# Second output projection of six channel groups as seven block products, with weight differences formed by GpSimd in layer 0

## The chip, the cores and the metric

The kernel runs on one core of one Trainium2 chip. The core has a matrix engine (TensorE, PE in the profile), a vector engine (VectorE, DVE), an engine for activation functions (ScalarE, ACT), a general engine (GpSimd, POOL) and a queue engine that issues DMA transfers (SyncE, SP). Each engine executes its own list of instructions in order, and they wait for each other by semaphores. Working memory is SBUF; matmuls write to PSUM, which has eight banks here, each 128 partitions of 512 float32. The metric is the device time of one execution in microseconds.

## The reference: what is computed

A two-layer encoder over 16 meta tokens and 256 input tokens of width 2048, all in float32, one sequence. Layer 0 mixes with gated linear attention and stick-breaking attention. Layer 1, the layer of this change, is a Mamba-2 mixer:

```python
proj = jnp.einsum('btd,de->bte', h, w_in)                 # 2048 -> 10304
z, xbc, dt_raw = _split(proj, ODD_SPLITS)
xbc = jax.nn.silu(_causal_depthwise_conv(xbc, conv_w, conv_b))
...
y = _ssd(xs, bs, cs, dt, a_log, d_skip)                   # 4096 channels in 8 groups of 512
y = _rms_norm_groups(y * jax.nn.silu(z), norm_w, SSM_GROUPS)
return jnp.einsum('bte,ed->btd', y, w_out)                # 4096 -> 2048
```

After it come the residual and a layer norm. The change concerns the last einsum, the output projection: for each of the eight groups the 256 kept tokens times 512 channels are multiplied with a block of 512 x 2048 of `w_out`, and the eight results are added.

## The kernel before

**Number format.** Matmuls run on `float32r` operands. To keep float32 accuracy each operand is split in a high part (an ACT copy to `float32r`, L159) and a residue (a subtraction, L160, on DVE or on POOL), and each product is three matmuls: high x high, high x low, low x high (`three`, L176 to 180). Weights arrive as `raw` tiles of 128 x 2048 (1 MB), three buffers; each half of 1024 columns is split into a pair of tiles `whi` and `wlo`, five buffers each. `split_half` (L162) gives the second half of every third unit of layer 1, from unit 24 on, to POOL.

**Units.** The work is a list of weight units, `L0` with 104 and `L1` with 112. An input unit of layer 1 (`in_unit`, L182) computes 128 output channels for all tokens: 16 k-tiles times three matmuls of up to 272 columns, in four quarters of 12. For each SSM group g there are ten: B, C, four of x, four of z. An output unit (`out1_unit`, L505) multiplies group g's 512 channels with 512 columns of `w_out`: two token halves times four k-tiles times three matmuls of 128 x 512, so 24, into two PSUM banks, and then two DVE instructions (L503) scale each bank by the RMS factor `rr` of its tokens (tokens lie on partitions there) and add it to `acc`. `L1` is ssd(0), ssd(1), and then for g = 2 to 7 ssd(g) followed by out1(g - 2), and at the end out1(6) and out1(7).

**Side work.** After each quarter of an input unit, and at four places of an output unit, `tick` (L109) lets every pending generator emit its next step. `post_*` reads a finished unit from PSUM; for B, C and x it is the convolution (`conv`, L1062: one ACT instruction and three of DVE, all reading the PSUM bank). `decay1` (L1099) prepares the decay matrix `M`, and `mix_ssd` (L1236) does the chunk matmuls, multiplies with the SiLU gate on POOL (L1266), weights and splits the result into `yh` and `yl` (L1268, L1269; two buffers each) and computes the RMS factor (L1279 to 1289). `tail` (L1292) runs the last five output units with the layer norm, all of token half 0 before half 1.

**What sets the order.** Instructions are recorded in the order of the code; a planner then orders every engine's list by that order as a priority and by a simulated readiness. `post_*` and additions to `acc` are recorded with raised priority. `pin` keeps the order among some matmuls, and `keep_order` that of DVE and ACT at the end. Weight loads, the small round trips of `to_tokens` in layer 0 (L594) and the broadcast of decays (L1089) all go through SP's queue. PSUM has four banks `pj` for unit results, two `po` and two `z` for side work.

## Time and profile before

Three runs gave 1382.5, 1382.53 and 1383.26 us, median 1382.53. The page shows one profiled execution; it gives the span from its first to its last instruction, and no time of its own for that execution.

| what | value |
|---|---|
| median of the runs | 1382.53 us |
| profiled execution, span | 1385.0 us |
| profiled execution, own time | not given on the page |
| PE busy | 1374.1 us (99%) |
| DVE busy | 1030.8 us (74%) |
| ACT busy | 768.3 us (55%) |
| POOL busy | 263.1 us (19%) |
| DMA | 256.73 MB, mean 185 GB/s |

A line of the page's instruction groups names the code line, the engine, the operation, the tiles written and read, the shape and the count, then the busy time and the mean duration of one, then the idle time of the engine just before it and what ended it. The stretch from 0 to about 679 us is layer 0, the rest layer 1; group 7's last input unit ends at about 1305 us. PE's durations are those of pipelined instructions, so that the distance between two starts, and not the length of one, is what a matmul costs.

### The profile page before, as it was taken

How to read it: one execution, taken by the hardware profiler on the slowest of the kernel's cores; microseconds unless marked ns; L12 is line 12 of the kernel's file. 1: busy time of each engine (PE TensorE's matmuls, PEld its weight loads, DVE VectorE, ACT ScalarE, POOL GpSimd, SP SyncE). 2: the span in 40 equal slices, each digit the busy share in tenths (PEclk: the TensorE clock that was granted, in tenths of full speed). 3: DMA queues.
4: the chain of work that ended last, by engine and by line, in shares of the span. 5: the costliest groups of instructions: out<-in, count | busy, mean ns of one | idle time of the engine just before them, and what ended most of it. 6: DMA issues, size and time to landing. Idle time of an engine off the chain costs nothing.

```text
span 1385.0 us, 26232 instructions
## 1 busy us (share of the span) xinstructions
PE 1374.1 (99%) x10643; PEld 1323.9 (96%) x10643; DVE 1030.8 (74%) x1762; ACT 768.3 (55%) x1141; POOL 263.1 (19%) x253
## 2 busy tenths in 40 slices
PE   9999999999999999999999999999999999999998
PEld 8999999999999999999999999899898999989986
DVE  7858576576565674568899999787877778867687
ACT  6646455355345544556587667656565655656551
POOL 0000100100101100004401143331322323133221
PEclk9999999999999999999999999999999999999999
DMA  9656446546455545554355655465555555455561
GB/s 329 209 172 201 163 163 206 169 155 227 153 173 171 169 161 191 172 165 161 123 183 197 231 181 205 169 244 182 209 177 195 190 191 222 169 198 183 181 214 61
DMA packets 61945, 256.73 MB, mean 185 GB/s; under 512 B 26176, under 2 KB 29056, under 8 KB 33408
## 3 DMA queue, kind: packets, MB, share of 16 engines
q1 hardware_dynamic: 61104, 254.27, 53.3%
q8 instruction: 83, 1.36, 0.4%
q10 hardware_dynamic: 720, 0.79, 0.2%
q14 instruction: 38, 0.31, 0.1%
HBM read 249.29 MB, written 5.74 MB: 184 GB/s over the span
## 4 chain that ended last, share of the span: by engine, by line
PE 94%; DVE 4%; DMA 1%; issue 1%; POOL 0%; ACT 0%; SPq 0%; ACTq 0%; DVEq 0%; POOLq 0%
PE pj L179 25%; PE pj L178 25%; PE pj L180 25%; PE pj L494 4%; PE pj L496 4%; PE pj L495 4%; PE po L1255 1%; PE po L631 1%; DVE wlo L160 1%; PE po L1193 0%; DMA raw<-in_wts 0%; DVE M L1125 0%; PE z L1143 0%; DVE xt L1070 0%; DVE acc L503 0%
## 5 line engine op out<-in xcount | busy, mean ns | idle before, releaser
L178 PE MATMUL pj<-xhi,whi 128*128 128x272 f32 (+4 forms) x2560 | 732.1, 286 | 1.7 <-ACT xhi L330 0.8
L179 PE MATMUL pj<-xlo,whi 128*128 128x272 f32 (+4 forms) x2560 | 730.8, 286 | 0.0
L180 PE MATMUL pj<-xhi,wlo 128*128 128x272 f32 (+4 forms) x2560 | 730.1, 286 | 0.0
L159 ACT ACTIVATE whi<-raw 128x1024 fp32r<-128x1024 f32 (+2 forms) x434 | 449.2, 1039 | 398.3 <-PE pj L179 326.3
L160 DVE TENSOR_TENSOR wlo<-raw,whi 128x1024 fp32r<-128x1024 f32 (+2 forms) x405 | 503.4, 1247 | 209.6 <-ACT whi L159 199.6
L178 PEld LDWEIGHTS pj<-xhi,whi 128*128 128x128 f32 x2560 | 482.6, 189 | 4.3 <-ACT whi L159 1.1
L179 PEld LDWEIGHTS pj<-xlo,whi 128*128 128x128 f32 x2560 | 482.6, 189 | 1.2 <-issue 0.6
L180 PEld LDWEIGHTS pj<-xhi,wlo 128*128 128x128 f32 x2560 | 482.6, 189 | 0.8 <-issue 0.8
L178 PE MATMUL pj<-mixh,whi 128*128 128x272 f32 x384 | 111.0, 290 | 0.0
L180 PE MATMUL pj<-mixh,wlo 128*128 128x272 f32 x384 | 110.7, 289 | 0.0
L179 PE MATMUL pj<-mixl,whi 128*128 128x272 f32 x384 | 110.7, 288 | 0.0
L160 POOL TENSOR_TENSOR wlo<-raw,whi 128x1024 fp32r<-128x1024 f32 x29 | 73.1, 2520 | 193.7 <-ACT whi L159 193.7
L494 PE MATMUL pj<-whi,yh 128*128 128x512 f32 (+1 forms) x240 | 93.3, 389 | 0.0
L495 PE MATMUL pj<-wlo,yh 128*128 128x512 f32 (+1 forms) x240 | 92.6, 386 | 0.0
L496 PE MATMUL pj<-whi,yl 128*128 128x512 f32 (+1 forms) x240 | 92.2, 386 | 0.0
L261 POOL TENSOR_TENSOR gr<-gr,gsc 128x1088 f32<-128x1088 f32 x6 | 15.4, 2574 | 303.6 <-ACT gsc L260 303.6
L179 PEld LDWEIGHTS pj<-mixl,whi 128*128 128x128 f32 x384 | 72.4, 188 | 0.2
L180 PEld LDWEIGHTS pj<-mixh,wlo 128*128 128x128 f32 x384 | 72.3, 188 | 0.0
L178 PEld LDWEIGHTS pj<-mixh,whi 128*128 128x128 f32 x384 | 72.2, 188 | 0.2
L503 DVE SCALAR_TENSOR_TENSOR acc<-pj,rr,acc 128x512 f32<-128x512 f32 (+1 forms) x65 | 46.5, 733 | 13.9 <-PE pj L496 13.9
L496 PEld LDWEIGHTS pj<-whi,yl 128*128 128x128 f32 x240 | 45.1, 188 | 9.2
L494 PEld LDWEIGHTS pj<-whi,yh 128*128 128x128 f32 x240 | 45.1, 188 | 8.9
(347 smaller groups left out, 1462.4 us busy)
## 6 DMA issues: line engine op xcount, KB each, us to landing
raw<-in_wts SPq DMA_DIRECT2D x212, 1024.0 KB, 4.8
ebc<-edr SPq DMA_DIRECT2D x8, 1664.0 KB, 6.4
raw<-in_wts SPq DMA_DIRECT2D x9, 256.0 KB, 6.3
vdr<-vt SPq DMA_DIRECT2D x8, 256.0 KB, 5.2
vt<-vdr SPq DMA_DIRECT2D x32, 64.0 KB, 2.4
hacc<-in_xT SPq DMA_DIRECT2D x7, 272.0 KB, 5.3
early<-in_wts SPq DMA_DIRECT2D x2, 512.0 KB, 7.7
vdr<-vt SPq DMA_DIRECT2D x8, 128.0 KB, 3.4
```

The source lines that it names most:

```text
L159: self.nc.scalar.activation(hi, src, AF.Copy)
L160: eng.tensor_tensor(lo, src, hi.bitcast(F32), op=ALU.subtract)
L178: mm(ps, whi, xhi, start=first, stop=False)
L179: mm(ps, whi, xlo, start=False, stop=False)
L180: mm(ps, wlo, xhi, start=False, stop=last)
L261: mul(c, c, e, op=ALU.mult)
L494: mm(ps, yh[:, kk, tt], hi[:, k, :], start=kk == 0, stop=False)
L495: mm(ps, yh[:, kk, tt], lo[:, k, :], start=False, stop=False)
L496: mm(ps, yl[:, kk, tt], hi[:, k, :], start=False, stop=kk == 3)
L503: self.nc.vector.scalar_tensor_tensor(a, ps, r[:, t : t + 1], a, op0=ALU.mult, op1=ALU.add)
L631: mm = lambda r, a, b, start=False, stop=False: self.nc.tensor.matmul(o[:, r], a, b, start=start, stop=stop, skip_group_check=True)
L1255: pin(mm(ov[p][i * 64 : (i + 1) * 64, jj, t0:S], xd[:, s, h * 64 : (h + 1) * 64], M[:, h, c0:c1], start=(s, jj) == (0, 0), stop=False, **gk,))
```

## The change

For groups 0 to 5 the output projection is done by Strassen's scheme in Winograd's form. For a group and a half q of the 2048 output columns, `y` (256 tokens x 512 channels) and the weights (512 x 1024) are cut into 2 x 2 blocks. With A the blocks of `y` and B those of the weights, seven products replace eight: A11 B11, A12 B21, S2 T2, S3 T3, S1 T1, (-A22) T4 and S4 B22, where S1 = A21 + A22, S2 = S1 - A11, S3 = A11 - A21, S4 = A12 - S2, and T1 = B12 - B11, T3 = B22 - B12, T2 = B22 - T1, T4 = T2 - B21. Each product is 128 x 256 times 256 x 512, six matmuls of 128 x 512. There are 6 x 2 x 7 = 84 products.

- **Order of units.** `L1` is now ssd(0) to ssd(7) without a break, then out1(6) and out1(7). The products stand between quarters of the input units: the first of group g after quarter 64 + 40 g of layer 1 (unit 16 + 10 g), the others 20/7 quarters apart. Each product is followed by one addition to `acc`.
- **Weight differences.** The blocks lie in DRAM a second time, in the order B11, B12, B22, B21 (`_pack`). In layer 0 a generator `quad_sums` loads 24 tiles of 1 MB through SP, forms T1 to T4 in place by four subtractions of 128 x 512 each on POOL, and stores the tile to DRAM through SP.
- **Loads and splits.** `product_load` reads 0.5 MB per product into one of two buffers, two products ahead. `product_split` splits them a product ahead into the `whi` and `wlo` tiles, now six of each; the residue is formed on POOL for the four products with T, on DVE for the three others.
- **Left side.** Because blocks of different tokens are added, the RMS factor is applied to `y` before the products: the sum of squares is broadcast over partitions by a matmul of ones with 256 columns, and the factor, 128 x 256 now, comes out of Ln, Exp and a Newton step. `seven_parts` multiplies `y` with weight and factor (DVE), forms the S on POOL and splits A11, A12, -A22 and the S on ACT and DVE. Groups 6 and 7 keep the old form with `plain_parts` and `weighted`.
- **PSUM.** The four `pj` banks get names of their own. From unit 6 of layer 1 until the tail, banks 0 and 1 serve the units in turn and banks 2 and 3 the products.
- **Room.** `hacc` becomes two tiles, `ones` a view of `ones_r`, `yu` goes, and 128 bytes remain of the scratch for descriptors.

```diff
-    l1 = ssd(0) + ssd(1)
-    for g in range(2, NG):
-        l1 += ssd(g) + out1(g - 2)
+    l1 = [u for g in range(NG) for u in ssd(g)]
     l1 += out1(NG - 2) + out1(NG - 1)
...
+NS7 = 6
+LEFT = ((("aah", "aal"), 4, P), (("anh", "anl"), 2, P), (("ssh", "ssl"), 4, S))
+SEVEN = (
+    ("a11", 0, False, 0, True, (0, 0)),
+    ("a12", 3, False, 1, True, (0, 0)),
+    ("s2", 2, True, 0, False, (1, 0)),
+    ("s3", 1, True, 1, True, (1, 1)),
+    ("s1", 0, True, 0, False, (1, 1)),
+    ("n22", 3, True, 1, False, (1, 0)),
+    ("s4", 2, False, 0, False, (0, 1)),
+)
+PRODUCTS = [(g, q, n) for g in range(NS7) for q in range(2) for n in range(7)]
+PROD_AT = {64 + 40 * (k // 14) + (k % 14) * 20 // 7: k for k in range(len(PRODUCTS))}
...
     def pj(self):
-        return self.pp.tile([P, 512], F32, tag="pj", name=self.nm("pj"), bufs=4)
+        self.pjn += 1
+        return self.bank(self.pjs[self.pjn % len(self.pjs)])
...
             self.tick()
+            if 4 * (i - len(L0)) + q in PROD_AT:
+                self.product(PROD_AT[4 * (i - len(L0)) + q])
...
+    def quad_sums(self):
+
+        nc, sub = self.nc, self.nc.gpsimd.tensor_tensor
+        for g in range(NS7):
+            for q in range(2):
+                d = self.sums[g, q] = self.tc.dram_tile([2, P, 2048], F32, name=self.nm("qs"))
+                for c in range(2):
+                    b = self.lp.tile([P, 4, 512], F32, tag="quad", name=self.nm("quad"))
+                    flat = b.rearrange("p a c -> p (a c)")
+                    nc.sync.dma_start(flat, self.quad_rows(g, q)[c])
+                    for _ in range(5):
+                        yield
+                    for o, x, y in ((0, 1, 0), (1, 2, 1), (2, 2, 0), (3, 2, 3)):
+                        sub(b[:, o, :], b[:, x, :], b[:, y, :], op=ALU.subtract)
+                        yield
+                    for _ in range(2):
+                        yield
+                    nc.sync.dma_start(d[c], flat)
+                    for _ in range(2):
+                        yield
+
+    def product_load(self, k):
...
+        src = self.sums[g, q] if is_sum else self.quad_rows(g, q)
+        src = src.rearrange("c p (s x) -> p c s x", s=4)[:, :, slot, :]
+        pool, tag = ((self.lp, "praw"), (self.hp, "hacc2"))[k % 2]
+        self.praw[k] = pool.tile([P, 2, 512], F32, tag=tag, name=self.nm("praw"))
+        self.nc.sync.dma_start(self.praw[k], src)
+
+    def product_split(self, k):
...
+        self.pparts[k] = self.split(raw, 1024, self.nc.gpsimd if is_sum else self.nc.vector)
+
+    def product(self, k):
...
+        while name not in self.left[g]:
+            self.tick()
+        yh, yl = self.left[g][name]
+        hi, lo = [a.rearrange("p (k c) -> p k c", k=2) for a in self.pparts.pop(k)]
+        if first and (n < 2):
+            self.pbank[bank] = self.bank(2 + bank)
+        ps = self.pbank[bank]
+        f = first
+        for j in range(2):
+            for a, b in ((yh, hi), (yh, lo), (yl, hi)):
+                mm(ps, a[:, j, :], b[:, j, :], start=f, stop=(j == 1 and a is yl), skip_group_check=True)
+                f = False
+        dq = 2 * q + c
+        a = self.acc[:, t, dq * 512 : (dq + 1) * 512]
+        with self.tc.high_priority():
+            self.nc.vector.tensor_tensor(a, a, ps, op=ALU.add)
+        self.pdone = k + 1
+        self.product_load(k + 2)
+        self.product_split(k + 1)
...
+        self.pjs = (0, 1)
+        for k in range(2):
+            self.product_load(k)
+        self.product_split(0)
         self.units(len(L0), L1[:-5], {n: None for n in range(NFIRST)})
...
+    def seven_parts(self, y, r, g):
...
+        for j in range(4):
+            vec.scalar_tensor_tensor(y[:, j, :], y[:, j, :], self.col(C_ON, 4 * g + j), r, op0=ALU.mult, op1=ALU.mult)
...
+        self.split_into(y[:, :, :P], h, l, vec)
...
+        act(h, a22, AF.Copy, scale=-1.0)
+        vec.scalar_tensor_tensor(l, a22, -1.0, h.bitcast(F32), op0=ALU.mult, op1=ALU.subtract)
...
+        tt(a22, a21, a22, op=ALU.add)
+        tt(a21, a11, a21, op=ALU.subtract)
+        tt(a11, a22, a11, op=ALU.subtract)
...
+        tt(a12, a12, a11, op=ALU.subtract)
...
+        self.split_into(y, h, l, vec)
...
+        if g < NS7:
+            mm(ps[:, :S], self.ones, sq, start=True, stop=True)
+            m, r = [lp.tile([P, S], F32, tag="ys2", name=self.nm("ys2"), bufs=2) for _ in range(2)]
+            vec.tensor_scalar(m, ps[:, :S], 1.0 / 512, RMS_EPS, op0=ALU.mult, op1=ALU.add)
+            act(r, m, AF.Ln)
+            act(r, r, AF.Exp, scale=-0.5)
+            self.newton(r, m, sq)
+            self.tasks["parts", g] = self.push(self.seven_parts(y, r, g))
```

More of the change, by code (lines that the diff above doesn't have):

```diff
@@ L86, in _wait, with __init__, __getitem__ @@
             yield
+class _TwoTiles:
+    def __init__(self, a, b):
+        self.a, self.b, self.n = a, b, a.shape[1]
+    def __getitem__(self, index):
+        p, k, t = index
+        k0 = k.start if isinstance(k, slice) else k
+        if k0 < self.n:
+            return self.a[p, k, t]
+        return self.b[p, slice(k.start - self.n, k.stop - self.n) if isinstance(k, slice) else k - self.n, t]
 class _Body:
@@ L97, in __init__ @@
         self.uid = 0
+        self.pdone, self.left = 0, {g: {} for g in range(NS7)}
+        self.pjs, self.pjn = (0, 1, 2, 3), 0
+        self.sums = {}
     def nm(self, s):
@@ L154, in part_tiles @@
         return [
-            self.wp.tile([P, 1024 + WO], F32R, tag=n, name=self.nm(n), bufs=5)[:, off : off + 1024] for n in ("whi", "wlo")
+            self.wp.tile([P, 1024 + WO], F32R, tag=n, name=self.nm(n), bufs=6)[:, off : off + 1024] for n in ("whi", "wlo")
         ]
```

105 lines of the change are left out of this document (87 added, 18 removed).

## The prediction

> **What bounds the kernel now.** I read the page's busy shares and chain first, then the stretches of the span, then single instructions.
>
> ```profile
> span 1385.0 us, 26232 instructions
> PE 1374.1 (99%) x10643; PEld 1323.9 (96%) x10643; DVE 1030.8 (74%) x1762; ACT 768.3 (55%) x1141; POOL 263.1 (19%) x253
> PE 94%; DVE 4%; DMA 1%; issue 1%; POOL 0%; ACT 0%; SPq 0%; ACTq 0%; DVEq 0%; POOLq 0%
> ```
>
> TensorE (PE) is the bound: it is idle 1385.0 - 1374.1 = 10.9 us in all. Only a matmul taken away, or a stall taken away, shortens the run. The columns of the next view are the stretch, its length, then busy us and (instructions) of PE, PEld, DVE, ACT, POOL, the granted clock, DMA share and GB/s.
>
> ```profile
> 100.00:600.00 500.00, 500.00 (x4048) 498.34 (x4048) 322.04 (x558) 246.42 (x355) 41.23 (x61) 1.00 0.53 178
> 679.00:787.40 108.40, 107.57 (x880) 103.95 (x879) 102.07 (x194) 78.51 (x131) 7.79 (x6) 1.00 0.55 192
> 787.40:879.40 92.00, 89.94 (x760) 88.41 (x760) 81.69 (x152) 62.66 (x100) 36.24 (x27) 0.98 0.55 197
> 879.40:904.60 25.20, 25.20 (x138) 20.37 (x137) 20.87 (x33) 14.07 (x18) 5.88 (x5) 1.00 0.48 172
> 904.60:1245.20 340.60, 340.60 (x2566) 320.68 (x2565) 263.40 (x415) 200.52 (x281) 95.60 (x71) 1.00 0.55 195
> 1245.20:1305.20 60.00, 60.00 (x506) 59.92 (x505) 45.35 (x70) 35.94 (x51) 15.06 (x12) 1.00 0.53 183
> ```
>
> The rows are the middle of layer 0; the first 16 input units of the second layer; the next 14; the output projection of group 0; four whole groups (ten input units and four output units each); the ten input units of group 7. In the four groups one group takes 340.60 / 4 = 85.15 us of PE, 65.85 of DVE (VectorE), 50.1 of ACT, 23.9 of POOL (GpSimd). Up to 879 DVE is at 94% and 89%, and PE is not fed in full: 14 units at the pace of the last row would be 84.0, they took 92.0.
>
> **The saving on PE.** An old output unit has 24 matmuls of 128x512, so 96 a group; seven products times two column halves times six matmuls are 84. Twelve a group go, 72 in all.
>
> ```profile
> 969.13 0.39 PE L494 MATMUL pj<-whi,yh 128*128 128x512 f32 x1
> ...
> 970.94 0.39 PE L496 MATMUL pj<-whi,yl 128*128 128x512 f32 x1
> ```
>
> Eight matmuls start in 1.81 us, one every 0.2263 (the 0.39 is pipelined length). 72 x 0.2263 = 16.3 us, 2.72 a group: 85.15 becomes 82.43. The ones-matmul of the RMS grows from two of 16 columns to one of 256; I take it as 0, bounds -0.2 and +0.3 a group.
>
> **What DVE, ACT and POOL gain.** Columns here: busy us, mean ns | idle before.
>
> ```profile
> L160 DVE TENSOR_TENSOR wlo<-raw,whi 128x1024 fp32r<-128x1024 f32 x94 | 121.0, 1290 | 55.8 <-ACT whi L159 52.3 <-PE pj L180 3.4
> L503 DVE SCALAR_TENSOR_TENSOR acc<-pj,rr,acc 128x512 f32<-128x512 f32 x33 | 23.6, 740 | 6.0 <-PE pj L496 6.0
> L1125 DVE TENSOR_SCALAR M<-ebc,est 128x256 f32<-128x256 f32 x32 | 15.2, 474 | 5.6 <-PE po L1255 5.6
> L1269 DVE SCALAR_TENSOR_TENSOR yl<-yu,cpk,yh 128x256 fp32r<-128x256 f32 x16 | 12.9, 832 | 0.3 <-ACT yh L1268 0.3
> L1077 DVE TENSOR_SCALAR xcl<-xt 128x544 f32<-128x544 f32 x8 | 7.6, 948 | 0.2
> L1077 DVE TENSOR_SCALAR xcl<-gz 128x512 f32<-128x512 f32 x8 | 3.4, 420 | 0.0
> L449 DVE TENSOR_TENSOR hacc<-hacc,pj 128x272 f32<-128x272 f32 x80 | 34.1, 431 | 10.5 <-PE pj L180 10.0
> L160 POOL TENSOR_TENSOR wlo<-raw,whi 128x1024 fp32r<-128x1024 f32 x19 | 48.9, 2573 | 115.8 <-ACT whi L159 115.8
> L1266 POOL TENSOR_TENSOR yu<-yu,gz 128x256 f32<-128x256 f32 x16 | 13.9, 885 | 47.4 <-DVE yu L1265 47.4
> L1081 POOL TENSOR_TENSOR gz<-gz,xcl 128x512 f32<-128x512 f32 x8 | 11.4, 1425 | 45.9 <-ACT xcl L1080 45.9
> L159 ACT ACTIVATE whi<-raw 128x1024 fp32r<-128x1024 f32 x112 | 118.2, 1058 | 111.3 <-PE pj L179 65.8 <-PE pj L496 38.0 <-issue 3.5
> ```
>
> Per group, on DVE, taking 0.08 us of each duration as overlapped with its neighbour (the durations of the L160 and L503 rows add up to more than their share of the union): weight splits, 23.5 before; after, 20 halves of the input units less 3.3 that POOL keeps, plus the 6 products on plain blocks: 22.7, so -0.9. Accumulations: eight of 0.66 become fourteen; a plain add of 512 from PSUM is 431 ns x 512/272, less fixed cost, about 0.61: +3.2. Left parts: four multiplications and three residues of 512, 256 and 1024 (about 3.7) for four yl (1.6): +2.1. The RMS on 128x256 instead of 128x2: +0.7. Sum +5.1. ACT: six more splits of 1.06, and small ones: +7, to 57 of 82 us, no bound. POOL: eight product splits for 1.3 fewer others, 6.7 x 2.4 = +16.1, and four block sums of 256 elements at 0.75: +3.0. POOL goes from 23.9 to 43.0.
>
> DVE and POOL do not run freely beside each other:
>
> ```profile
> L1125 DVE TENSOR_SCALAR M<-ebc,est x64: 334/343/2557, 769.3 to 1235.4; 128x256 f32<-128x256 f32 x64
> L1269 DVE SCALAR_TENSOR_TENSOR yl<-yu,cpk,yh x32: 462/482/2258, 796.1 to 1337.3; 128x256 fp32r<-128x256 f32 x32
> L160 DVE TENSOR_TENSOR wlo<-raw,whi x405: 406/1225/2782, 5.7 to 1352.0; 128x1024 fp32r<-128x1024 f32 x130, 128x512 fp32r<-128x512 f32 x3, 128x256 fp32r<-128x256 f32 x2
> ```
>
> Mean less median is what is lost: 94 x 0.065 + 32 x 0.131 + 16 x 0.35 + 8 x 0.50 (L1077, against 0.42 x 544/512) = 19.9 us in four groups, 5.0 a group, 0.21 us of DVE for a POOL us. DVE is busy 77% of the time there; where it is never idle I take 0.21 / 0.77 = 0.27, bounds 0.21 and 0.65. So 19.1 more POOL us cost DVE 5.2, and it comes to 65.85 + 5.1 + 5.2 = 76.1 of 82.43: 92%. The cover is then only 6 us a group, and I give back 0.9 of the 2.72 (bounds 0 and 5, below): -1.8 for each of groups 1 to 5, together **-9**.
>
> The Trainium skill, SBUF — State Buffer, section Who interferes with whom, says the second port pair of DVE is an exclusive lock with GpSimd: an instruction with two SBUF inputs waits for a whole GpSimd instruction that reads SBUF. The long maxima above agree; a full block at every meeting would make the price the 0.65 of the third rival, where the rows show 0.21.
>
> **Group 0.** From 787.4 to 904.6, 117.2 us, PE lost 8.0. DVE was busy 81.7 + 20.9 = 102.6; added are -0.9, +3.2, the left parts of two groups (2 x 2.8) and 8 x 2.4 + 2 x 3.0 = 25.2 POOL us at 0.27 = 6.8: 117.3. DVE is now the bound there and the group's 2.72 is lost: **0**, bounds -8 (those stalls go) and, above, from the first product's own chain:
>
> ```profile
> 804.23 0.69 POOL ysq L1275
> 805.00 1.37 POOL ysq L1275
> 806.41 0.62 PE po L1281 x4
> ```
>
> In the chain of waits group 0's sum of squares reached PE at 806.4. Behind it now come Ln, Exp, the Newton step, weighting and a split, some 6 us by the rows above, so product 0 cannot run before about 812; its place in the code is unit 16, which began at 787.4. The planner may let PE go on with input units meanwhile, as many as two banks allow; where it misjudges the chain by 6 us, PE stands 6: **+6** is the upper bound.
>
> **PSUM banks.** Two of the four pj banks now belong to the products, so an input unit must wait until the unit two before it was read out.
>
> ```profile
> 765.41 0.56 ACT L1066 ACTIVATE xt<-pj,cpk 128x272 f32<-128x272 f32 x1
> ...
> 777.22 0.48 DVE L1070 SCALAR_TENSOR_TENSOR xt<-pj,cpk,xt 128x269 f32<-128x269 f32 x1
> ```
>
> ```profile
> 1021.32 0.56 ACT L1066 ACTIVATE xt<-pj,cpk 128x272 f32<-128x272 f32 x1
> ...
> 1029.47 0.89 DVE L1070 SCALAR_TENSOR_TENSOR xt<-pj,cpk,xt 128x270 f32<-128x270 f32 x2
> ```
>
> The convolution's reads end 12.3 and 9.0 us after ACT's first; a unit lasts 60.0 / 10 = 6.0 us, with a product or so in it 1.9 more. Four banks hide both. Two leave 6.3 in the first case, where no product runs yet. DVE's order is made anew with the two banks known, and PE's later waits at 787 to 879 shrink by what it waited earlier: **+2**, bounds 0 and +6.3.
>
> **Layer 0.** 96 subtractions of 512 at 1.3 us are 125 us of POOL beside 322 of 500 us of DVE: at 0.21 us each 26 us more, to 70%, which idle time holds. 48 transfers of 1 MB are added to SP's queue, and stores wait there for POOL, loads for the store, weight loads behind both.
>
> ```profile
> SPq L144 <- DVE wlo L160: 609.5, 140, 10.4
> ```
>
> ```profile
> raw<-in_wts SPq DMA_DIRECT2D x212, 1024.0 KB, 4.8
> ```
>
> A weight load starts when DVE frees its buffer, about two units (12 us) before its use, and lands in 4.8: 7 us of cover against some 5 for a store. 0.53 of the DMA engines' time becomes some 0.74. **+0.5**, bounds 0 and +4; without the cover each of 24 stores would cost up to 5.
>
> **The end.** Output units of groups 6 and 7 follow the last input unit at once; before, group 5's 25 us stood between.
>
> ```profile
> 1315.38 0.87 DVE L1265 SCALAR_TENSOR_TENSOR yu<-xt,cpk,po 128x256 f32<-128x256 f32 x2 [1.30 <-PE po L1261]
> ...
> 1336.88 1.35 DVE L1269 SCALAR_TENSOR_TENSOR yl<-yu,cpk,yh 128x256 fp32r<-128x256 f32 x2
> ```
>
> Group 7's parts were done 33 us after 1305.2, but that chain paused for buffers of groups 5 and 6 that no longer stand in its way; from 1315.4 it needs some 6 us, so about 16 after the last unit. PE needs them after three units and a half, 12 x 1.36 + 3.4 + 2.7 = 22. The two banks also serve these units, and an add of 0.74 must fit into 1.36 us: **+1.5**, bounds 0 and +4.
>
> **Sum:** -9 + 0 + 2 + 0.5 + 1.5 = **-5.0 us**. The page gives the span (1385.0) and no own time of that execution; it lies 2.5 over the median of the runs, so I take the change off the median: 1382.5 - 5.0 = 1377.5, say **1378**.
>
> **Rivals.** (1) DVE keeps up and nothing else shows: -16.3 and some 2 at the end, 1368; for it, 6 us of cover a group; against it, bursts in which DVE lags 9 us already. (2) DVE's lost time takes all: group 84.7 instead of 82.4, 1382.5. It needs 0.4 us lost for a POOL us rather than 0.27: 70.95 - 5.0 + 0.4 x 43.0 = 83.2 of DVE, over PE's 82.43. (3) The full lock: 0.65 of DVE's time is in instructions with two SBUF inputs, as I judge the rows; 66 + 0.65 x 43.0 = 94 us a group, +8.8 in five, 1426. The trace of before speaks against it: by the same count it would have 76 of DVE where it has 65.85. (4) **Slower: the two banks.** The 9.0 us lag grows with DVE's load, 92% for 77%, to 10.8, with 1.1 until ACT's read 11.9; 7.9 is hidden, 4 stay, once a group. Five groups are +20, the first stage +6.3, group 0 keeps nothing of its 2.7, the end +2: -16.3 + 20 + 6.3 + 2.7 + 2 = +14.7, 1397; with 3 a group 1392. It decides from 2.7 a group on. Against it: the read-out has priority in the order.
>
> **Chances.** The forecast (-3 to -10) 0.37; rival 1 (beyond -10) 0.13; rival 2 or another balance within 2.8 us 0.20; the banks 0.22; the lock or a late transfer in layer 0 0.08. Faster by over 0.2% (2.8 us, about what a measurement of this kernel can tell) 0.50, no difference 0.20, slower 0.30. The range goes from 1366, just past the whole saving, to 1395, most of the banks' case. The forecast's own range is 1372 to 1380.
>
> **What would show it.** 504 matmuls of 128x512 on the products' line at 0.226 us; a group of 83 to 84 us between equal units, against 85.15; DVE at 90% or more there and POOL near 43 us a group; L160 on DVE further over its median. If PE's idle time names DVE's convolution (L1070's successor) before an input unit's first matmul, the banks decide and I am wrong; if it names wlo on POOL before a product, POOL's chain does. Layer 0 should keep its length: its last matmul within 4 us of where it was.

## The result, and the profile after

The changed kernel takes **1526.18 us** (median of 4 runs, 1524.58 to 1530.46) against 1382.51 (4 runs, 1381.9 to 1383.26): a ratio of 1.1043, 95% interval 1.1026 to 1.106. It is slower by 144 us, where 1378 was forecast and the range ended at 1395.

The page of the changed kernel: span, busy time of each engine, the granted clock in 40 slices, and the shares of the chain of waits.

```profile
span 1522.9 us, 26579 instructions
...
PE 1401.1 (92%) x10559; PEld 1340.8 (88%) x10559; DVE 1183.1 (78%) x1812; ACT 800.3 (53%) x1171; POOL 556.3 (37%) x413
...
PEclk9999999899899999999979999898998999989999
...
PE 50%; DVE 18%; DMA 13%; issue 6%; POOL 6%; ACT 4%; SPq 1%; ACTq 0%; POOLq 0%; DVEq 0%
```

Fewer matmuls run, as the change says (10643 to 10559; 72 of these are the products'). But PE, which had 94% of the chain, has 50% now; it is idle 121.8 us where it was idle 10.9, and slices with a clock below full speed have appeared. The time is lost in three places, not in one. The next view gives stretches of the changed kernel: the first layer without its beginning, units 0 to 9 of the second layer, units 10 to 29, and the groups 3 to 6 (columns as in the prediction).

```profile
27.00:500.00 473.00, 442.53 (x3483) 438.53 (x3475) 335.70 (x506) 216.20 (x309) 191.54 (x134) 0.96 0.75 272
720.30:809.30 89.00, 68.86 (x547) 67.54 (x545) 75.34 (x150) 62.16 (x108) 1.29 (x1) 0.88 0.49 177
809.30:991.50 182.20, 163.31 (x1211) 152.81 (x1210) 156.69 (x231) 101.29 (x142) 75.12 (x52) 0.95 0.55 191
991.50:1380.90 389.40, 351.91 (x2510) 325.27 (x2509) 334.73 (x447) 221.82 (x300) 190.87 (x113) 0.94 0.59 201
```

The same first stretch before, in which PE was never idle:

```profile
27.00:500.00 473.00, 473.00 (x3846) 470.32 (x3838) 316.16 (x556) 238.37 (x345) 38.55 (x50) 1.00 0.54 181
```

| stage (ends at the first matmul of an input unit) | before | after | difference |
|---|---|---|---|
| first layer, to unit 0 | 678.8 | 720.3 | +41.5 |
| units 0 to 29 (before: and group 0's output units) | 225.8 | 271.2 | +45.4 (some 3.5 of it is other work) |
| four groups, units 30 to 69 | 340.6 | 389.4 | +48.8 |
| the rest, to the end | 139.8 | 142.0 | +2.2 |
| span | 1385.0 | 1522.9 | +137.9 |

The profiled execution of the kernel before was some 4 us longer than its executions beside the runs below (spans of 1380.5 to 1381.3), so the stages add up to 137.9 and not to 144. The work of two stages isn't the same on both sides. In units 0 to 29 the run with three banks below, which has the changed kernel's matmuls, keeps PE busy for 226.4 us, the kernel before for 222.9. In the rest 48 fewer matmuls of 128x512 stand (eight products and two groups' output units in place of three groups'), 40 small ones of the chunks more, and PE is idle 12.0 us there in place of 5.7: the +2.2 hides a loss.

What PE waits for in the four groups stands in its groups of instructions (busy us, mean ns | idle before, and what ended it):

```profile
L214 PE MATMUL pj<-xhi,whi 128*128 128x272 f32 (+2 forms) x640 | 187.3, 293 | 13.3 <-DVE xt L1184 10.5 <-DVE bc L1184 2.7
...
L216 PE MATMUL pj<-xhi,wlo 128*128 128x272 f32 (+2 forms) x641 | 185.4, 290 | 1.6 <-DVE wlo L192 1.6
L614 PE MATMUL pj<-wlo,ssh 128*128 128x512 f32 x64 | 27.4, 428 | 7.0 <-DVE wlo L192 7.0
L614 PE MATMUL pj<-whi,ssh 128*128 128x512 f32 x64 | 27.3, 427 | 15.7 <-DVE acc L619 15.7
```

13.3 us before input units (their bank is not yet read by the convolution, L1184), 8.6 for a residue, 15.7 before a product (its bank is not yet added, L619): every one of them ends with VectorE. Together 37.6 us, which is all of PE's idle time there (389.4 - 351.9 = 37.5).

### The profile page after: what moved, and what is told of

Same layout as the page of the kernel before. It is cut to its first block, busy times and chain, and to the rows that moved or that the text cites. A ratio compares the mean times of both kernels' runs of the same rounds, so it can differ in the third digit from the quotient of the medians.

```text
span 1522.9 us, 26579 instructions
## 1 busy us (share of the span) xinstructions
PE 1401.1 (92%) x10559; PEld 1340.8 (88%) x10559; DVE 1183.1 (78%) x1812; ACT 800.3 (53%) x1171; POOL 556.3 (37%) x413
## 4 chain that ended last, share of the span: by engine, by line
PE 50%; DVE 18%; DMA 13%; issue 6%; POOL 6%; ACT 4%; SPq 1%; ACTq 0%; POOLq 0%; DVEq 0%
PE pj L214 14%; PE pj L216 14%; PE pj L215 14%; DVE wlo L192 4%; POOL quad L573 4%; DMA quad<-in_wts 4%; PE pj L614 3%; DMA praw<-qs 3%; ACT whi L191 2%; DVE M L1267 2%; DMA qs<-quad 2%; DMA vdr<-vt 2%; DVE M L1239 2%; DMA vt<-vdr 1%; PE po L739 1%
## 5 line engine op out<-in xcount | busy, mean ns | idle before, releaser
L214 PE MATMUL pj<-xhi,whi 128*128 128x272 f32 (+4 forms) x2560 | 742.2, 290 | 29.2 <-DVE xt L1184 12.3
L191 ACT ACTIVATE whi<-raw 128x1024 fp32r<-128x1024 f32 (+2 forms) x386 | 395.9, 1033 | 270.6 <-PE pj L215 206.2
L573 POOL TENSOR_TENSOR quad<-quad 128x512 f32<-128x512 f32 x96 | 154.1, 1605 | 256.0 <-DMA quad<-in_wts 222.2
L192 POOL TENSOR_TENSOR wlo<-praw,whi 128x1024 fp32r<-128x1024 f32 x48 | 125.8, 2623 | 125.5 <-ACT whi L191 112.7
L191 ACT ACTIVATE whi<-praw 128x1024 fp32r<-128x1024 f32 x84 | 88.4, 1053 | 89.1 <-PE pj L614 41.3
L216 PE MATMUL pj<-mixh,wlo 128*128 128x272 f32 x384 | 112.7, 294 | 0.0
L1195 POOL TENSOR_TENSOR gz<-gz,xcl 128x512 f32<-128x512 f32 x16 | 28.8, 1801 | 165.6 <-ACT xcl L1194 165.6
L192 POOL TENSOR_TENSOR wlo<-raw,whi 128x1024 fp32r<-128x1024 f32 x21 | 55.0, 2617 | 47.5 <-ACT whi L191 47.4
L614 PE MATMUL pj<-whi,ssh 128*128 128x512 f32 x96 | 41.5, 432 | 27.8 <-DVE acc L619 25.5
L619 DVE TENSOR_TENSOR acc<-acc,pj 128x512 f32<-128x512 f32 x84 | 56.8, 677 | 12.5 <-PE pj L614 12.2
L1192 ACT ACTIVATE xcl<-xcl 128x544 f32<-128x544 f32 (+2 forms) x40 | 25.5, 639 | 60.0 <-DVE xcl L1191 60.0
```

The source lines that it names most:

```text
L191: self.nc.scalar.activation(hi, src, AF.Copy)
L192: eng.tensor_tensor(lo, src, hi.bitcast(F32), op=ALU.subtract)
L214: mm(ps, whi, xhi, start=first, stop=False)
L216: mm(ps, wlo, xhi, start=False, stop=last)
L573: sub(b[:, o, :], b[:, x, :], b[:, y, :], op=ALU.subtract)
L614: mm(ps, a[:, j, :], b[:, j, :], start=f, stop=(j == 1 and a is yl), skip_group_check=True)
```

## The experiments

The theories: **lock** (VectorE held while GpSimd reads SBUF), **queue** (GpSimd's list in order: loads that have not landed, or long work ahead of what others need), **banks** (two PSUM banks for the input units, one each for two products), **transfers**, and **the first product's early load**. Each kernel was timed once beside the kernel before (1382.2 to 1383.0 us). The changed kernel's own four runs lie within 6 us, and its first layer ends between 720.3 and 727.3 in the five kernels here that share its code, so a single difference of that size decides nothing.

**The first layer: subtractions or transfers?** One edit takes the subtractions out:

```diff
-                    for o, x, y in ((0, 1, 0), (1, 2, 1), (2, 2, 0), (3, 2, 3)):
-                        sub(b[:, o, :], b[:, x, :], b[:, y, :], op=ALU.subtract)
+                    for _ in range(4):
                         yield
```

> The changed kernel without the 96 subtractions of weight blocks on GpSimd in the first layer; the 24 loads and 24 stores of 1 MB stay, so the stored blocks are plain copies and the products get wrong weights. In the trace after, the first layer is 42 us longer than before. Theory GpSimd's queue (subtractions that wait for a load hold the causal selects and gates behind them, and the long subtractions hold VectorE): without them the first layer is at most 10 us longer than before, the run is near 1492. Rival transfers (48 MB more on the DMA engines, stores that hold weight loads on SyncE's queue): the first layer stays 30 us or more too long, the run stays above 1512.

Another takes the whole pass out:

```diff
-        self.push(self.quad_sums())
...
-        src = self.sums[g, q] if is_sum else self.quad_rows(g, q)
+        src = self.quad_rows(g, q)
```

> The changed kernel without the whole pass over the weight blocks in the first layer: no loads, no subtractions, no stores; the products read the plain blocks, so the weight differences are left out. Everything in the second layer keeps its shape. Theory of independent places: the 42 us of the first layer go, the second layer keeps its loss, the run is 1484 within 4. Rival common cause (the second layer is slow because of what the first leaves behind, or because the sums must be read back from memory just written): the second layer gets shorter too, the run falls below 1475. The second layer's loss alone is then 1484 - 1382.5 = about 100 us.

Measured: 1490.75 and 1492.51 us; the first layer ends at 685.0 and 683.4. The subtractions cost 35 us, the transfers without them nothing that shows, although DMA's share is 0.75 in the changed kernel and 0.54 before. 1492.5 is 8 above the 1484 expected for it: the first layer keeps 5 of its 42 us, and the rest is some 4 longer. The second layer keeps its loss: a second cause.

**Queue or lock in the first layer.** The first attempt was to record the subtractions four steps later:

```diff
-                    for _ in range(5):
+                    for _ in range(9):
                         yield
```

> The changed kernel with nine steps of the side work between a weight block's load and its subtractions in place of five, so that the load has landed when GpSimd comes to them; same work, nothing left out. The pass then runs to about 620 us in place of 483. Theory queue: the first layer's 33 us come from GpSimd standing at a load that has not landed with causal selects and gates behind it; without that wait at least 20 of them go, the run is 1505 or less. Rival lock or length: the subtractions cost by their 1.36 us and VectorE's port, wherever they stand; the run stays at 1518 or more.

1529.08 us, but the edit didn't do what it was meant to: each engine's list is ordered anew by the planner, and GpSimd's group of subtractions still waited for the loads. First the changed kernel's row, then this one's:

```profile
L573 POOL TENSOR_TENSOR quad<-quad 128x512 f32<-128x512 f32 x96 | 154.1, 1605 | 256.0 <-DMA quad<-in_wts 222.2 <-DMA vt<-vdr 28.5
L573 POOL TENSOR_TENSOR quad<-quad 128x512 f32<-128x512 f32 x96 | 153.7, 1601 | 270.5 <-DMA quad<-in_wts 263.8 <-issue 1.7
```

So it says nothing on the queue. The next kernel loads one block once and subtracts in it 96 times; nothing is stored:

```diff
+            if n == 0:
+                b = self.lp.tile([P, 4, 512], F32, tag="quad", name=self.nm("quad"))
+                nc.sync.dma_start(b.rearrange("p a c -> p (a c)"), self.quad_rows(g, q)[c])
...
-                    nc.sync.dma_start(d[c], flat)
```

> The changed kernel with the 96 subtractions of the first layer on one block that is loaded once: GpSimd does all of them, with no later load to wait for and no store; the products read plain blocks (the weight differences are left out). Recording the subtractions later had not taken GpSimd's wait away (263.8 us still ended with the load). Theory queue: with nothing to wait for, the first layer keeps at most 10 of its 33 us, the run is 1500 or less. Rival length and lock: GpSimd's 130 us beside VectorE cost by themselves, the first layer keeps 25 us or more, the run is 1515 or more.

1547.91 us: with nothing to wait for, the first layer is longer still, 740.5. So a loss of this size needs no wait for a load. GpSimd now runs 30 subtractions in one go, and VectorE's timeline beside it (start, us, instruction) reads:

```profile
43.05 10.37 DVE L438 SCALAR_TENSOR_TENSOR hacc<-hacc,shiftc 128x544 f32<-128x544 f32 x6
53.34 0.49 DVE L643 TENSOR_SCALAR gm<-po,cpk 128x272 f32<-128x272 f32 x1
53.75 3.07 DVE L438 SCALAR_TENSOR_TENSOR hacc<-hacc,shiftc 128x544 f32<-128x544 f32 x2
56.74 0.43 DVE L758 TENSOR_SCALAR gr<-pj 128x272 f32<-128x272 f32 x1
```

GpSimd in the same kernel:

```profile
39.90 50.20 POOL L571 TENSOR_TENSOR quad<-quad 128x512 f32<-128x512 f32 x30
```

And the kernel before at the same place:

```profile
43.96 0.49 DVE L540 TENSOR_SCALAR gm<-po,cpk 128x272 f32<-128x272 f32 x1
44.37 1.35 DVE L398 SCALAR_TENSOR_TENSOR hacc<-hacc,shiftc 128x544 f32<-128x544 f32 x2
45.64 0.43 DVE L655 TENSOR_SCALAR gr<-pj 128x272 f32<-128x272 f32 x1
```

A multiply-add with two SBUF inputs takes 10.37 / 6 = 1.73 us in place of 0.68, which is the pace of GpSimd's subtractions (50.2 / 30 = 1.67): the two engines take turns, one for one. Instructions that read PSUM (gm from po, gr from pj) keep their 0.49 and 0.43. An instruction with one SBUF input isn't safe either: later in the same stretch two casts of 16x128 between SBUF tiles take 1.19 and 1.26 us, 0.22 and 0.21 in the kernel before. Of the 46.9 us that PE waits between 27 and 300 us in this run, 40.1 end with VectorE.

In the changed kernel most of PE's waits in the first layer are others. Of 30.5 us of idle time between 27 and 500 us, 20.1 come before the matmuls of one line (the row gives the sum, the times and the longest):

```profile
PE po L739 <- ACT s0h L680: 20.1, 4, 8.5
```

The longest ends at 292.5 us, and this is what stood before it:

```profile
278.27 0.53 ACT L828 ACTIVATE spad<-z 128x432 f32<-128x432 f32 x1 [4.05 <-PE z L825]
285.92 5.28 POOL L573 TENSOR_TENSOR quad<-quad 128x512 f32<-128x512 f32 x4 [11.72 <-DMA quad<-in_wts]
291.15 0.68 POOL L288 TENSOR_SCALAR_AFFINE_SELECT spad<-spad 128x128 f32<-128x128 f32 x3
291.86 0.56 ACT L680 ACTIVATE s0h<-spad 128x432 fp32r<-128x432 f32 x1 [8.77 <-POOL spad L288]
```

The input of the causal selects is ready at 278.8 us, and they start at 291.15: ahead of them in GpSimd's list stand four subtractions that wait for their load until 285.92 and then take 5.28 us. The wait that ends at 402.0 has the same cause (ready at 390.8, selects at 400.66), and so has a short one at 101.7. These three are 16.5 of the 30.5 us, and they are the queue's; in the kernel before the selects start 0.07 to 0.13 us after their input. So the first layer shows both causes, in the changed kernel more of the queue, in the run without waits more of the lock.

The Trainium skill, SBUF — State Buffer, section Who interferes with whom, has it so: a VectorE instruction with two SBUF inputs against a GpSimd instruction that reads SBUF, and not against one that only writes. The timeline above agrees on the first half. By the second half a GpSimd that only writes would cost little. That could be tried in both layers at once:

```diff
-                    for o, x, y in ((0, 1, 0), (1, 2, 1), (2, 2, 0), (3, 2, 3)):
-                        sub(b[:, o, :], b[:, x, :], b[:, y, :], op=ALU.subtract)
+                    for o in (0, 2, 0, 2):
+                        nc.gpsimd.memset(b[:, o : o + 2, :], 0.0)
                         yield
...
+            for _ in range(2):
+                self.nc.gpsimd.memset(lo.bitcast(F32), 0.0)
```

> The changed kernel in which GpSimd keeps every place in its queue and every wait, but only writes: each of the 96 subtractions is a memset of 128x1024 of the same block after the same load, each of the 48 residues two memsets of 128x1024 into the same tile that the matmuls then read (weight sums and their low parts are left out). The Trainium skill (SBUF - State Buffer, Who interferes with whom) has a GpSimd instruction that only writes stay clear of VectorE. Theory lock on SBUF reads: GpSimd is as long or nearly, but VectorE's two-input instructions keep their length beside it; both losses go together, the first layer keeps at most 12 of its 36 us and the groups fall to 84 to 88: about 1440 to 1470. Rival GpSimd's queue (loads that have not landed, long work ahead of what others need): with the waits in place both losses stay, 1510 or more.

**1445.82 us**: 80 us go. The first layer ends at 685.8, the four groups take 87.6, 87.4, 91.4 and 87.6. GpSimd still waits for the loads; the memsets in place of the residues wait for their buffer, and not for ScalarE's high part as the residues did (112.7 of their 125.5 us):

```profile
L601 POOL MEMSET wlo<- 128x1024 f32 x96 | 92.9, 974 | 61.0 <-PE pj L620 34.6 <-PE pj L216 24.3
L573 POOL MEMSET quad<- 128x1024 f32 x96 | 87.7, 958 | 274.3 <-DMA quad<-in_wts 274.3
```

It stood longer at the loads (274.3 us) than the changed kernel (222.2), and it cost nothing. But no causal select was held up either: here they start 2.1 us after their input once and 0.07 to 0.13 us otherwise, up to 500 us. The memsets are also shorter than what they replace (0.96 us for 1.60, 1.95 for 2.62). So in the first layer this run takes both causes away and doesn't say how much each had; that stays open. In the second layer the queue plays no part: in the four groups of the changed kernel none of PE's waits ends with GpSimd, and VectorE waits for GpSimd 1.3 us in all. There the lock is left, or TensorE's wait for the residues themselves; the next runs separate these.

**The second layer: the residues.** First without them, then with them formed but unused, then on VectorE:

```diff
-        self.pparts[k] = self.split(raw, 1024, self.nc.gpsimd if is_sum else self.nc.vector)
+        if is_sum:
+            hi, _ = self.part_tiles()
+            self.nc.scalar.activation(hi, raw, AF.Copy)
+            self.pparts[k] = hi, hi
```

> The changed kernel without the low parts of the 48 blocks of weight sums: GpSimd forms no residue for them, and the products use the high part twice (the matmuls stay, the low part's contribution is left out). GpSimd loses 126 us of the second layer, VectorE gains no work. Theory port lock (VectorE waits while GpSimd's back-to-back residues hold the shared port): the groups fall from 95 to 100 us to at most 87 us each, the run is 1465 or less. Rival two banks (input units and products wait for VectorE's read-outs because each has only two banks): the groups stay at 92 us or more, the run stays above 1495. In between, both count.

```diff
+        hi, lo = self.split(raw, 1024, self.nc.gpsimd if is_sum else self.nc.vector)
+        self.pparts[k] = (hi, hi) if is_sum else (hi, lo)
```

> The changed kernel with GpSimd forming all 48 residues of the weight sums exactly as before, but no matmul reading them: the products use the high part twice (as in the run without the residues; the low parts' contribution is left out). GpSimd's work and the port stay as in the changed kernel; only TensorE's wait for GpSimd's result is gone. Theory lock: the cost is VectorE held beside GpSimd, groups stay at 93 us or more, the run is 1510 or more. Rival late chain: TensorE waited for GpSimd's own long residues (2.6 us each, in order), the run falls to 1475 or less.

```diff
-        self.pparts[k] = self.split(raw, 1024, self.nc.gpsimd if is_sum else self.nc.vector)
+        self.pparts[k] = self.split(raw, 1024, self.nc.vector)
```

> The changed kernel with the residues of the 48 blocks of weight sums formed on VectorE in place of GpSimd (126 us of GpSimd become some 48 x 1.23 = 59 us of VectorE by the median of its residues); nothing is left out. Without those residues at all the run was 1466. Theory lock: what costs is the meeting of the two engines, VectorE's own 59 us cost less than the lock did (10 us a group on VectorE, which has some of that idle): 1475 to 1500. Rival: VectorE is full either way, its 59 us come on top of 1466 in full: 1525, no better than the changed kernel.

1466.16, 1532.2 and 1496.67 us. Without the residues 60 us go and the groups take 84.6 to 87.8. With the residues formed but read by no matmul, nothing goes at all: TensorE didn't lose its time by waiting for GpSimd's results. On VectorE they cost 30 us where on GpSimd they cost 60, although VectorE is the busier engine. The four groups in the run without residues:

```profile
980.30:1323.50 343.20, 334.74 (x2511) 313.41 (x2510) 284.80 (x448) 223.22 (x300) 106.73 (x81) 1.00 0.66 229
```

Against the changed kernel, GpSimd has 190.87 - 106.73 = 84.1 us less and VectorE, with the same instructions, 334.73 - 284.80 = 49.9 us less: **0.59 us of VectorE lost for a us of GpSimd**. Rows with both inputs in SBUF get shorter: the residues on VectorE (`wlo<-raw`, 106.0 to 87.3 us) and the multiplications of M (25.8 to 17.1). Rows with one input in PSUM stay: the additions to `acc` (37.9 and 38.1) and the convolution (23.5 and 23.6). Single instructions of the changed kernel show how:

```profile
1148.65 8.06 DVE L1267 TENSOR_TENSOR M<-M,cb 128x800 f32<-128x800 f32 x4 [0.42 <-POOL cb L288]
1156.63 2.71 DVE L1273 TENSOR_TENSOR mt<-mt,cb 16x32 f32<-16x32 f32 x4
1159.38 1.23 DVE L192 TENSOR_TENSOR wlo<-raw,whi 128x1024 fp32r<-128x1024 f32 x1
1160.52 0.68 DVE L619 TENSOR_TENSOR acc<-acc,pj 128x512 f32<-128x512 f32 x1
```

The shortest, median and longest (ns) of the four multiplications and of the four tiny ones:

```profile
L1267 DVE TENSOR_TENSOR M<-M,cb x4: 983/2061/3194, 1148.6 to 1153.6; 128x800 f32<-128x800 f32 x4
L1273 DVE TENSOR_TENSOR mt<-mt,cb x4: 171/178/2318, 1156.6 to 1159.2; 16x32 f32<-16x32 f32 x4
```

GpSimd meanwhile, and what came of it on PE:

```profile
1149.82 6.04 POOL L192 TENSOR_TENSOR wlo<-praw,whi 128x1024 fp32r<-128x1024 f32 x2 [1.06 <-ACT whi L191]
1155.82 3.09 POOL L192 TENSOR_TENSOR wlo<-raw,whi 128x1024 fp32r<-128x1024 f32 x1
...
1161.35 0.76 PE L614 MATMUL pj<-whi,ssh 128*128 128x512 f32 x1 [7.94 <-DVE acc L619]
```

The same multiplications in the four groups before (mean 987 ns):

```profile
L1153 DVE TENSOR_TENSOR M<-M,cb 128x800 f32<-128x800 f32 x16 | 14.9, 987 | 1.0 <-POOL cb L249 1.0
```

Three residues follow one another for 9 us, and each holds up one instruction of VectorE until it ends: two of the multiplications keep their 0.99 us and two take 3.2 and 3.1, one of the tiny ones takes 2.3 and the others 0.17 to 0.18. The add behind them in VectorE's list comes late, the product's one bank is not free, PE stands 7.94 us.

**The banks.** The bank rule alone, put on the kernel before (round-robin over named banks, two for input units), first with the old output units on the other two, then with these on all four:

```diff
+        return self.bank(self.pjs[self.pjn % len(self.pjs)])
...
+        self.pjs = (0, 1)
...
-        pst = [self.pj(), self.pj()]
+        pst = [self.bank(2), self.bank(3)]
```

> The kernel before with only the bank rule of the change: after the first units of the second layer, input units use two PSUM banks and the old output units the other two. Work, transfers and GpSimd stay as before. Forecast's term: +2 (bounds 0 and 6.3) on the whole, 1385 within 4. Rival two banks: 4 us or more a group and more in the first stage, 1400 or above. The run without GpSimd's residues still lost some 3 us a group and 20 us before unit 30, so the value in between, near 1395, is what this theory of two causes expects.

> The kernel before with two PSUM banks for the input units of the second layer, and the old output units rotating over all four in pairs (2 and 3, then 0 and 1). It takes the output units' own waits out of the run with two and two banks, which took 1468. Theory input units: the convolution's late read-out costs 4 us a group and some 10 before unit 20, and 4 us come from the fixed rotation in the first layer: near 1425. Rival: what cost in the run with two and two banks was the output units waiting for VectorE's adds, so this is within 1395.

1468.02 and 1428.83 us: 85 and 46 us slower without any of the change's work. In the first, output units too wait for VectorE's adds; that is 39 of the 85. The second is for the most part the price of two banks for the input units. Its four groups, 89.05 us each in place of 85.15, with VectorE's load as before:

```profile
L183 PE MATMUL pj<-xhi,whi 128*128 128x272 f32 (+2 forms) x640 | 182.9, 286 | 7.5 <-DVE xt L1077 3.4 <-ACT xt L1073 3.0 <-DVE rm L1293 1.0
```

By stage, against the profile of before: +8.3 in the first layer, +16.1 in units 0 to 29, +15.6 in the four groups, +2.1 at the end. So 34 us belong to the second layer, where the two banks are. The first layer has four banks as before and only takes them in fixed turns; why that costs 8 us there (5.0 of them in one wait for a residue, which ends at 53.5 us) is open.

**The first product.** Its load and split moved from the start of the second layer to quarters 52 and 60:

```diff
-        for k in range(2):
-            self.product_load(k)
-        self.product_split(0)
...
+            if 4 * (i - len(L0)) + q == 52:
+                self.product_load(0)
+                self.product_load(1)
+            if 4 * (i - len(L0)) + q == 60:
+                self.product_split(0)
```

> The changed kernel with the loads of the first two products recorded in quarter 52 of the second layer and the first split in quarter 60, in place of right after the first units of that layer. Theory: the first split stands in ScalarE's order ahead of the weight splits of units 7 and 8 and waits for a transfer whose buffer the residual frees late, and that costs the some 20 us between units 6 and 9: the run is near 1506. Rival: these 20 us come from the two banks or from dt's chain and stay, the run is 1520 or more.

1521.84 us, only 4 us less, though its own place got better: units 0 to 9 take 73.3 us in place of 89.0 (before: 65.2). In the changed kernel PE stood there twice:

```profile
781.11 0.84 PE L1169 MATMUL po<-ident,dt_scr 64*128 64x64 f32 x4 [12.94 <-DVE dt_scr L1160]
781.75 0.42 PE L1171 MATMUL po<-ident,dt_scr 64*16 64x64 f32 x2
788.71 0.58 PE L214 MATMUL pj<-xhi,whi 128*128 128x256 f32 x1 [6.54 <-ACT whi L191]
```

Both waits go with the edit. The second ends with the weight split that stands behind the product's in ScalarE's list (787.6 and 786.7 us), as was expected; how the first hangs on it is not shown. The 16 us are won in their place, but units 10 to 19 take 7 us longer, where PE now stands 8.3 us, 3.7 of them for the decay matrix on VectorE. The run as a whole is within the spread of the changed kernel.

**Everything out, then the banks back.** The three edits together (no pass in the first layer, first product late, no residues), then with four banks until quarter 52, then with three banks after it. The second and third edit are shown against the run before each:

> The changed kernel with three parts out at once: no pass over the weight blocks in the first layer (the products read plain blocks), the first product's load and split late, no residue on GpSimd (products use the high part twice). Weight differences and their low parts are left out. If the three losses are independent: 1524.5 - 33 - 4 - 60 = 1428. If they share a cause, or one hid behind another: 1410 or less. What is left above 1382.5 - 16.3 = 1366 is then the price of the two banks, of the first product's chain and of VectorE's own extra work.

```diff
-        self.pjs = (0, 1)
...
                 self.product_load(1)
+                self.pjs = (0, 1)
```

> As the run with all three parts out, and the input units keep four PSUM banks until quarter 52 of the second layer, where the first products are loaded; two from there on. Theory two banks in the first stage: 8 to 12 us less than that run, near 1418. Rival: the first stage's loss is VectorE's order or dt's chain, within 3 us of that run.

```diff
-                self.pjs = (0, 1)
+                self.pjs = (0, 1, 2)
...
-            self.pbank[bank] = self.bank(2 + bank)
+            self.pbank[bank] = self.bank(3) if bank else self.zb[1]
...
-        self.zi ^= 1
+        self.zi ^= len(self.pjs) != 3
+        if len(self.pjs) == 3:
+            self.zi = 0
```

> As the run with all three parts out and four banks until quarter 52 (1405.5), but from there the input units keep three banks: the products take one of the two banks of the M products (the other serves these alone) and one pj bank. Theory banks: the input units' waits for the convolution go, 1 to 2 us a group and 4 between units 16 and 30, the run is near 1393. Rival: what is left is the products' own two banks (a product waits until VectorE added the one before) and VectorE's load, within 4 us of 1405.

1414.74, 1405.54 and **1390.24 us**. The first lies between its two cases: the sum of the single effects (98 us) falls short of what they give together (111), which fits repairs that partly hide behind the next stall when each is made alone. The banks then give 9 and 15 us. In the last run the four groups are close to what the matmuls alone take:

```profile
683.20:916.30 233.10, 226.43 (x1756) 214.33 (x1755) 212.40 (x380) 163.05 (x249) 44.47 (x41) 1.00 0.62 217
916.30:1250.90 334.60, 332.95 (x2511) 313.51 (x2510) 290.02 (x448) 221.76 (x300) 100.96 (x81) 1.00 0.68 234
```

A group takes 83.65 us. That is 1.5 less than before, with weight sums and their residues for nothing; and this run still takes 8 us more than the kernel before. By stage it is 4.4 us longer in the first layer and 7.3 in units 0 to 29 (3.5 of it other work), and 6.0 shorter in the four groups.

**Repaired and whole.** Two kernels leave nothing out. One has the sums' blocks in halves with two buffers and the loads recorded ahead, residues on VectorE, the first product late and three banks; the other has whole blocks and all the arithmetic of the sums on VectorE:

```diff
-        nc, sub = self.nc, self.nc.gpsimd.tensor_tensor
+        nc, sub = self.nc, self.nc.vector.tensor_tensor
```

> The whole change, nothing left out, repaired where the runs point: the sums' blocks in column halves with two buffers and each load recorded one ahead, residues of the weight sums on VectorE, first product late, four banks until quarter 52 and three after. By the runs so far: 1526 - 29.5 (residues) - 10 to 20 (banks and first product) - 0 to 28 (first layer): 1450 to 1485. It would have to come under 1382 to be worth anything; no theory here expects that. Above 1485 the repairs hide behind one another.

> The whole change, nothing left out, with all of the weight sums' arithmetic on VectorE: the 96 subtractions of the first layer and the 48 residues of the second; first product late, four banks until quarter 52, three after. The second layer is that of the repaired run (1477, of which the first layer with its half blocks had 59). Theory lock: 96 x 0.7 = 67 us more of VectorE in the first layer fit its idle third, the first layer is at most 20 us longer than before: 1420 to 1438. Rival: VectorE's order now has the loads in it and stands at them, the first layer is 35 us or more longer: 1453 or more.

1477.22 and **1431.58 us**. The first gains in the second layer and loses it in the first, which got 59 us too long. There the queue is at work again: the longest wait of PE, 14.5 us, ends at 309.6 behind causal selects that were ready at 291.0 and started at 308.3, after eight of the 192 smaller subtractions, which had waited 10.3 us for a load. The second is the best whole version, 1.035 of the time before. Its VectorE rows in the first layer:

```profile
L579 DVE TENSOR_TENSOR quad<-quad 128x512 f32<-128x512 f32 x96 | 68.6, 715 | 50.5 <-DMA quad<-in_wts 49.8
```

VectorE does in 68.6 us what GpSimd did in 154.1, and even stands 49.8 us at loads, and the first layer is 18 us too long instead of 41.5. GpSimd's list holds no subtractions here, so queue and lock go together once more. No version came under the kernel before.

## Why the prediction was wrong

Run by run the 144 us come apart like this: 111 go with the three parts out, 9 and 15 more with banks given back, and 8 are left. Forecast was a gain of 5.

- **PE's saving** was right in kind: of the 2.72 a group that were forecast, PE's busy time shows 1.9 in the run with three banks, where the other causes are out (332.95 / 4 = 83.2 in place of 85.15), and the group's length 1.5.
- **The lock's price is the step that failed first; the -9 for groups 1 to 5 hangs on it.** The forecast took 0.27 us of VectorE for a us of GpSimd, within 0.21 and 0.65, from mean less median in the trace of before. The runs show 0.59, near the upper bound, and without the residues on GpSimd 60 us go. The counts beside it held: VectorE without the added loss 65.85 + 5.1 = 70.95 us a group, measured 284.80 / 4 = 71.2; GpSimd 43.0, measured 47.7. What was missed is that the rows of before priced GpSimd instructions that stand apart; of three residues in a row each holds up one instruction of VectorE until it ends. The third rival, the full lock with 94 us a group, was nearest to the four groups' 97.35 and had been given a part of 0.08.
- **The cover of an average.** VectorE's 76.1 of 82.43 was taken as "6 us of cover", 0.9 a group given back. With 83.7 of 97.35 VectorE is 86% busy and PE still waits 9.4 us a group: what is late is a single read-out or add behind blocked instructions. A share below 100% is no cover for a chain with one buffer.
- **PSUM banks: +2, bounds 0 and 6.3, was too small by more than ten times.** The kernel before loses 46 us by that rule alone, 34 of them in the second layer, and 3.9 in each of the four groups. The fourth rival had said 4 a group, but only once VectorE's load had grown; at the old load it was thought to be hidden. "Four banks hide both", read from two places, was no measure for two. The products' own banks, one each, were not priced at all: PE's largest wait in the four groups, 15.7 us, is theirs.
- **Layer 0: +0.5, bounds 0 and 4, came out at +41.5.** The forecast had 26 us of VectorE lost there, "which idle time holds", and saw the danger in stores and loads on SP's queue. The transfers alone cost nothing; the subtractions cost 35 us. GpSimd's own list wasn't looked at: the causal selects that PE's matmuls of linear attention wait for stand in it behind subtractions that wait for loads, and at least 16.5 of PE's 30.5 us of waits there come from that. VectorE held by the lock has a part too, and the run without waits shows that it can cost more; how large it is in the changed kernel is open. The rest, 6, is what the fixed turn of the banks can cost by the run with the bank rule alone (8).
- **Group 0 and units 0 to 29: 0, bounds -8 and +6, came out at +45.4.** The chain of the first product was looked at from unit 16 on; that its load and split are recorded right after the first units and stand ahead of the weight splits of units 7 and 8 was not (16 us in their place). Another part is the two banks before any product runs: four banks until quarter 52 gave 9 us. The residues are a third: without them units 20 to 29 take 87.5 us in place of 101.2.
- **The end: +1.5, measured +2.2**, is no hit: the stage has 48 matmuls of 128x512 less, 10.9 us at 0.2263, and only part of that is filled by 40 chunk matmuls of another group; PE is idle 6.3 us more in it.

The forecast's mechanism for "slower" existed twice among the rivals, each alone and each with one place. In the changed kernel they came together, and neither was given the first layer.

## What to carry to other kernels

Work moved to GpSimd beside a VectorE that is 75% busy isn't free work: price it by what VectorE does between SBUF tiles, at up to one for one while GpSimd runs without a pause, and compare it with simply giving VectorE the work (30 us against 60 here, 68.6 us of work against 154.1). Then look at what stands behind the new work in GpSimd's own list, and at what that work waits for: here it was causal selects behind a load. A buffer that is taken away must be priced with the latest read-out in the trace and not with the mean load, and by a run of the old kernel with that rule alone: it would have shown 46 us here. A saving of 1 to 2% of the matmuls must leave every other engine's lateness as it was.

## What the runs showed of the hardware that was not expected

- **The price of a stall goes on after it.** PE in the run with subtractions that never wait, before and after two waits (10.42 us, two matmuls, then 6.78 us):

```profile
44.51 0.29 PE L214 MATMUL pj<-xhi,whi 128*128 128x272 f32 x1
44.63 0.28 PE L215 MATMUL pj<-xlo,whi 128*128 128x272 f32 x1
...
64.89 0.60 PE L216 MATMUL pj<-xhi,wlo 128*128 128x272 f32 x1 [6.78 <-DVE wlo L192]
65.29 0.43 PE L214 MATMUL pj<-xhi,whi 128*128 128x272 f32 x1
65.51 0.43 PE L215 MATMUL pj<-xlo,whi 128*128 128x272 f32 x1
...
69.59 0.39 PE L215 MATMUL pj<-xlo,whi 128*128 128x272 f32 x1
69.82 0.29 PE L216 MATMUL pj<-xhi,wlo 128*128 128x272 f32 x1
```

  A matmul starts every 0.12 us before the waits and every 0.226 us after them (20 from 65.29 to 69.59), until 69.6: 4.7 us at about half speed, some 2 us lost on top of the waits. In the four groups of the changed kernel PE is busy 351.91 us at a clock of 0.94, in the run with three banks 332.95 at 1.00 for the same matmuls: of the 54.8 us between these two, 19 are this. The Trainium skill, TensorE: Matmul & The Clock Gate, Part 1, names a clock that is halved after an idle window of about 3.4 us and comes back after a busy one of that length; by that rule the stalls of 7 us cost a half-speed window each, and the trace, with 4.7 us at half speed, fits it roughly.
- **Small instructions pay the same.** A multiplication of 16x32 elements, 0.17 to 0.18 us otherwise, took 2.3 us beside a residue of GpSimd and ended with it: what it waits for has nothing to do with its own size. The mean of the four (0.68 us) shows none of this.
- **A GpSimd that never stands can cost more.** With 222 us of standing at its loads the first layer ended at 720.3, with none at 740.5. The same subtractions were spread over some 450 us in the first case and over 200 in the second (26.9 to 225.8). The standing wasn't free either, since the causal selects stood with it.
- **Writes seem not wholly free beside VectorE.** In the run with GpSimd's memsets VectorE's `M<-ebc,est` of 128x144 took 0.75 us on average in the four groups, 0.49 in the run without residues.
